# A two-layer hybrid block kernel whose issue order is planned by its own recorder instead of the scheduler

## The chip, the core and the metric

The kernel runs as one launch on one core of a Trainium2 chip. The metric is device microseconds of that launch. Five engines take part, each with its own in-order instruction queue: TensorE (PE in the profile) multiplies, VectorE (DVE), ScalarE (ACT) and GpSimd (POOL) do elementwise work, and SyncE (SP) issues the DMAs. An instruction at the head of a queue that waits for another engine holds up everything behind it on its own engine.

## The reference

The model is a diffusion block of two layers on 512 tokens and 256 context tokens, width 1024, feed-forward width 4096. Layer 1 carries no context queries. What is computed, cut to its skeleton:

```python
for each of the 2 layers:
    shift1, scale1, gate1, shift2, scale2, gate2 = silu(c) @ mod_w + mod_b     # for x and for the context
    h = modulate(rmsnorm(x), shift1, scale1)
    u = h @ w_in                                                              # split over four mixers
    y = concat(ssd_mixer(u), diff_mixer(u), gqa_mixer(u), mla_mixer(u))       # 256 columns each
    x = x + gate1 * (y @ w_out)
    h = modulate(rmsnorm(x), shift2, scale2)
    x = x + gate2 * (square(relu(h @ w1)) @ w2)
return rmsnorm(x) * final_norm_g
```

The four mixers are a chunked state-space scan in both directions, a differential attention (two softmaxes subtracted), a grouped-query attention and a latent attention, each with four heads; the three attentions run over 768 keys (context and tokens).

## The kernel before

Activations are held transposed, 128 features by 768 tokens, in eight tiles. Each large product is kept near float32 by splitting both factors into a high and a low part, and summing three products: high by high, high by low, low by high. `split` makes the parts of a weight: a copy on ScalarE (line 393), then a subtraction on VectorE or GpSimd (line 394). All products go through `mm` (line 198), transposes are on line 765.

The tiles named below: `pv` are the value projections, `pdk`, `pdq`, `pgb`, `pcqx` and their like the other input projections (`p` and the column group), `d_`, `g_` and `m_` the three attentions, with `_s` scores, `_t` transposed probabilities, `_o` outputs; `pe`, `pg`, `py`, `pst`, `hs` belong to the scan; `p` alone is the feed-forward. `pm`, `pn`, `pk` and `pl` are the modulation: `pm` multiplies the condition by a block of `mod_w` in four column groups of 32, `pn` sums the four, line 282 adds the bias into `modT`, line 366 forms the gain, lines 555 to 561 apply gain and shift and leave `xn` in high and low parts, which `pv` multiplies. Line 275 copies `pm` out of PSUM as `ms`. `pk` (loaded as `mk`) is the same for the later modulation columns of layer 0, spread between other work.

Products with a 64- or 32-column weight (`_o`, `pk`, `pm`, `py`, `pst`, `pg`) use part of the array's columns each (the profile writes 128*64 and 128*32); all others use it in full (128*128).

Stages in time: the start (norm, first modulation, value projections) to 58.5 us; projections and mixers of layer 0, with its modulation columns, to about 520; output projection and feed-forward of layer 0 to about 1100, beside which VectorE computes layer 1's modulation (line 312); the same for layer 1, mixers from about 1200 to 1510, feed-forward to the end, then the final norm (`nf_`, line 1425) and the store. While the last feed-forward products run, line 1308 adds each to the residual `h`, emptying its PSUM tile, and `squares` sums the squares into `acc` (line 522, on GpSimd, the eighth and last on VectorE), from which `nf_ms` is multiplied.

What sets the order. In the mixers, several Python generators (attention, projections, scan, modulation) are interleaved by `Weave`, which steps the one whose clock is least; the weights of that clock stand in `TUNE`. The instructions so traced are then ordered by the framework's scheduler, which simulates the engines with its own durations, takes priorities from `high_priority(e[4])` in `Weave.run`, and gives out pool buffers as it goes. Two things are held by hand: the start, from the norm to the last `pv`, stands in a `manual_schedule` block for PE, ScalarE and VectorE; and `issue_after` keeps the `pk` products behind the last product traced. PSUM has two score tiles of 1024 columns (tag `S`) and four of 512 (tag `g`).

Of the kernel before, what the change touches and what calls it, by code (L numbers as in the profile page):

```python
# [12 lines left out]
F32R = mybir.dt.float32r  # L13
# [6 lines left out]
P = 128  # L20
D = 1024
KT = 8
# [46 lines left out]
    pass  # L69


class Weave:


# [43 lines left out]

@with_exitstack
def hybrid_block_kernel(ctx: ExitStack, tc: tile.TileContext, a: dict, out: bass.AP, dbg=None):  # L120
    nc = tc.nc
    nc.scalar.preload_act_table_set("natural_log_exp_and_others")

    sb = ctx.enter_context(tc.tile_pool(name="sb", bufs=1))
    pp = ctx.enter_context(tc.tile_pool(name="pp", bufs=1, space=PSUM))
    dp = ctx.enter_context(tc.tile_pool(name="dp", bufs=1, space=DRAM))

    NL, NSM, NP, NWR, NWS, NSD = 43, 4, 6, 7, 4, 3

# [64 lines left out]
    stt = nc.vector.scalar_tensor_tensor  # L194
    gtt = nc.gpsimd.tensor_tensor
    gts = nc.gpsimd.tensor_scalar
    def mm(*args, **kw):
        r = nc.tensor.matmul(*args, **kw)  # L198
        K.last = r.ins
        return r  # L200

    ld = nc.sync.dma_start

    def f(ap):
# [14 lines left out]


    ident = const("ident", [P, P])
    make_identity(nc, ident)
    ones = const("ones", [P, P])
    nc.gpsimd.memset(ones, 1.0)
    epsT = const("epsT", [P, 1])
# [90 lines left out]
    def mod_quads():  # L316
# [20 lines left out]
        for i in range(4 * n):  # L337
            load(i + 1)
            yield 1.6 if i % 4 == 0 else 0.8
            if i % 4 == 0:  # L340
                po = ps_g(f"pk{i}")
            with tc.issue_after(K.last):
                for k in (2 * (i % 4), 2 * (i % 4) + 1):
                    w = ws.pop((i, k))
                    for g in range(4):
                        mm(po[32 * g : 32 * g + 32, 0:P], sil[:, k], w[:, P * g : P * g + P], start=k == 0, stop=k == KT - 1)
            if i % 4 == 3:
                m = sc(f"mq{i}", P)
                act(m, po[:, 0:P], AF.Copy)
                yield 0.2  # L350
                with tc.issue_after(K.last):
                    spread(i // 4, m)

    LO0 = nc.gpsimd.scalar_tensor_tensor
    LOP = ()
# [231 lines left out]
            except StopIteration as e:  # L587
                return e.value

    with tc.manual_schedule(engines={mybir.EngineType.PE, mybir.EngineType.Activation, mybir.EngineType.DVE}):  # L590
        for i, s in enumerate((XS, CS)):
            run(rstd_of(f"n1_0_q{i}", psq[i], rb, s))
        ws = [value_of(wv[0])]
        mod_done(0, mod_load(0))
        xn_start(0)
        ws.append(value_of(wv[1]))
        m = mod_load(1)
        mod_dma(3)
        next(wv[3])
        vps = v_start(0)  # L600
        for q in range(4):
            run(v_step(0, vps, ws[q], xn, 2 * q))
            if q < 3:
                mod_done(q + 1, m)
                xn_start(q + 1)
            if q < 2:
                ws.append(value_of(wv[q + 2]))
            run(v_step(0, vps, ws[q], xn, 2 * q + 1))
            if q < 2:
                m = mod_load(q + 2)  # L610


    tri = const("tri", [P, 2, P])
# [701 lines left out]
    for l in range(DEPTH):  # L1315
# [214 lines left out]
```

## Time and profile before

| | |
|---|---|
| median of 3 runs | 1863.81 us (1862.91 to 1869.71) |
| the profiled execution | 1864.9 us, of which the span is 1863.2 us |
| TensorE busy in the span | 1781.6 us, 96% |
| TensorE not busy | 81.6 us |
| mean granted TensorE clock | 0.982 of full speed |
| VectorE, ScalarE, GpSimd busy | 1088.6, 872.2, 465.8 us |

The profile is one execution. A busy time is the union of an engine's instructions; matmuls are pipelined, so a row's duration is longer than the distance to the next row, and the distance between two starts is what a matmul costs. The granted clock takes two values, full (2.4 GHz) and half (1.2 GHz), and a stretch's clock is their mean.

### The profile page before, as it was taken

Reading aid. Unit: us, or ns where it says so; the run is one execution under the profiler, and the core shown is the slowest. Engines: PE = TensorE matmul, PEld = TensorE weight load, DVE = VectorE, ACT = ScalarE, POOL = GpSimd, SP = SyncE. Lnnn points to the kernel's source line nnn. Section 1 sums busy time; section 2 is a strip of 40 time slices with the busy share of each in tenths; the row PEclk is TensorE's granted clock in tenths of the full one; section 3 lists DMA queues with packets and bytes.
Section 4 is the critical chain, followed back from the end, with each engine's and each line's share of the span. In section 5 each row is a group of like instructions: output and inputs, shape, how many; then the busy total and the mean of one; then the engine's idle time right before and its main releaser. Section 6 shows DMA issues by size and latency. Waiting matters only on the chain.

```text
span 1863.2 us, 30142 instructions
## 1 busy us (share of the span) xinstructions
PE 1781.6 (96%) x11206; PEld 1485.9 (80%) x11206; DVE 1088.6 (58%) x2112; ACT 872.2 (47%) x1776; POOL 465.8 (25%) x437
## 2 busy tenths in 40 slices
PE   7989999899999999999999999998899999999996
PEld 5777686677787988888888889787678998888885
DVE  5366856867485764543543265887986863333324
ACT  5245665767455313213213353676777652323242
POOL 2322322220134301101001674242211320101065
PEclk9989999999999999999999999999999999999998
DMA  9365422014345543432433334522014552332333
GB/s 356 106 166 162 111 74 62 27 25 150 95 131 153 174 138 97 151 126 91 147 125 100 127 119 116 137 73 65 13 48 152 168 166 91 96 96 92 96 119 102
DMA packets 117330, 216.28 MB, mean 116 GB/s; under 512 B 15424, under 2 KB 24640, under 8 KB 117184
## 3 DMA queue, kind: packets, MB, share of 16 engines
q1 hardware_dynamic: 117184, 214.36, 37.4%
q8 instruction: 88, 1.44, 0.3%
q14 instruction: 58, 0.48, 0.1%
HBM read 185.99 MB, written 8.13 MB: 104 GB/s over the span
## 4 chain that ended last, share of the span: by engine, by line
PE 82%; DVE 8%; ACT 4%; POOL 3%; issue 2%; DMA 1%; DVEq 0%; SPq 0%; POOLq 0%; ACTq 0%
PE p L198 45%; PE po L198 3%; PE pdk L198 2%; PE pv L198 2%; PE m_s L198 2%; PE pr L198 2%; PE m_o L198 2%; PE pdq L198 2%; PE d_o L198 2%; PE m_t L765 1%; PE g_o L198 1%; PE pk L198 1%; PE pxs L198 1%; PE g_s L198 1%; PE pe L198 1%
## 5 line engine op out<-in xcount | busy, mean ns | idle before, releaser
L393 ACT ACTIVATE w_0s<-w 128x512 fp32r<-128x512 f32 x256 | 160.9, 630 | 394.0 <-PE p L198 354.3
L1384 POOL TENSOR_TENSOR r<-r 128x512 f32<-128x512 f32 (+2 forms) x80 | 91.9, 1148 | 652.9 <-ACT a_0h L1383 387.9
L394 DVE TENSOR_TENSOR w_0s<-w,w_0s 128x512 fp32r<-128x512 f32 x216 | 150.6, 698 | 165.6 <-ACT w_0s L393 165.4
L312 DVE SCALAR_TENSOR_TENSOR junk<-mv,cb 128x512 bf16<-128x512 f32 x128 | 91.4, 718 | 117.6 <-DMA mv<-in_modw_dram 116.5
L1382 ACT ACTIVATE r<-p 128x512 f32<-128x512 f32 (+2 forms) x80 | 47.8, 597 | 168.6 <-PE p L198 166.9
L1308 DVE SCALAR_TENSOR_TENSOR h<-p,modT,h 128x512 f32<-128x512 f32 (+1 forms) x104 | 62.6, 624 | 102.2 <-PE p L198 102.2
L749 DVE TENSOR_REDUCE d_m<-d_s 128x1 f32<-128x768 f32 (+1 forms) x80 | 65.8, 842 | 33.4 <-PE d_s L198 33.3
L753 ACT ACTIVATE d_p<-d_s,d_m 128x768 f32<-128x768 f32 (+1 forms) x80 | 64.7, 812 | 35.6 <-DVE d_m L749 27.8
L394 POOL TENSOR_TENSOR w_0s<-w,w_0s 128x512 fp32r<-128x512 f32 x40 | 53.2, 1337 | 39.8 <-ACT w_0s L393 38.6
L522 POOL TENSOR_TENSOR acc<-acc,sq 128x256 f32<-128x256 f32 (+1 forms) x48 | 49.5, 1031 | 42.3 <-ACT sq L521 40.6
L198 PE MATMUL p<-xm_0h,w_0s 128*128 128x512 f32 (+1 forms) x176 | 55.1, 360 | 1.9 <-ACT r L1382 1.9
L198 PE MATMUL p<-a_0h,w_0s 128*128 128x512 f32 (+1 forms) x176 | 54.6, 356 | 0.9 <-DVE h L1308 0.5
L198 PE MATMUL p<-a_4h,w_0s 128*128 128x512 f32 (+1 forms) x176 | 54.6, 355 | 0.0
L198 PE MATMUL p<-xm_4h,w_0s 128*128 128x512 f32 (+1 forms) x176 | 54.6, 357 | 0.0
L198 PE MATMUL p<-xm_6h,w_0s 128*128 128x512 f32 (+1 forms) x176 | 54.5, 357 | 0.0
L198 PE MATMUL p<-xm_2h,w_0s 128*128 128x512 f32 (+1 forms) x176 | 54.4, 356 | 0.0
L198 PE MATMUL p<-a_2h,w_0s 128*128 128x512 f32 (+1 forms) x176 | 54.3, 355 | 0.0
L198 PE MATMUL p<-xm_7h,w_0s 128*128 128x512 f32 (+1 forms) x176 | 54.3, 356 | 0.0
L198 PE MATMUL p<-a_6h,w_0s 128*128 128x512 f32 (+1 forms) x176 | 54.3, 355 | 0.0
L198 PE MATMUL p<-xm_3h,w_0s 128*128 128x512 f32 (+1 forms) x176 | 54.3, 355 | 0.0
L198 PE MATMUL p<-xm_5h,w_0s 128*128 128x512 f32 (+1 forms) x176 | 54.2, 355 | 0.0
L198 PE MATMUL p<-a_7h,w_0s 128*128 128x512 f32 (+1 forms) x176 | 54.1, 353 | 0.0
(2380 smaller groups left out, 5625.0 us busy)
## 6 DMA issues: line engine op xcount, KB each, us to landing
w<-in_w_dram SPq DMA_DIRECT2D x320, 256.0 KB, 2.6
mv<-in_modw_dram SPq DMA_DIRECT2D x96, 256.0 KB, 2.7
mk<-in_modk_dram SPq DMA_DIRECT2D x64, 256.0 KB, 3.4
wr<-in_wout_dram SPq DMA_DIRECT2D x32, 256.0 KB, 2.8
h<-in_xT_dram SPq DMA_DIRECT2D x16, 384.0 KB, 7.5
mw<-in_mod_dram SPq DMA_DIRECT2D x16, 384.0 KB, 6.1
wo<-in_wout_dram SPq DMA_DIRECT2D x32, 192.0 KB, 2.4
wv<-in_wv_dram SPq DMA_DIRECT2D x16, 192.0 KB, 4.6
```

The lines of the kernel that those rows point to most:

```text
L198: r = nc.tensor.matmul(*args, **kw)
L312: stt(out=junk, in0=w, scalar=1.0, in1=cb[s, i], op0=ALU.mult, op1=ALU.mult, accum_out=m[:, 2 * i + s : 2 * i + s + 1])
L393: act(hi, src, AF.Copy)
L394: sub(out=lo, in0=src, in1=f(hi), op=ALU.subtract)
L522: (tt if k == KT - 1 else add)(out=acc[:, s], in0=acc[:, s], in1=q[:, s], op=ALU.add)
L749: nc.vector.tensor_reduce(out=u.m[:, 0:1], in_=u.ps[:, 0 : u.n], axis=AX.X, op=ALU.max, negate=True)
L753: act(u.p, u.ps[:, 0 : u.n], AF.Exp, bias=u.m[:, 0:1], accum_out=u.m[:, 1:2])
L765: nc.tensor.transpose(ps[:, i : i + P], u.p[:, b + i : b + i + P], ident)
L1308: stt(out=h[k][:, s], in0=ps, scalar=L.mod[:, mg + k, si : si + 1], in1=h[k][:, s], op0=ALU.mult, op1=ALU.add)
L1382: act(r, ps, AF.Relu)
L1384: gtt(out=r, in0=r, in1=r, op=ALU.mult)
```

## The change

Every engine and pool is replaced by a recorder. An operation is not issued where the program states it, but written down as an `Op` with the operations it must follow, found from the overlap of the tile areas read and written, and with the tiles it needs. Consecutive products into one output tile are joined into one operation as long as their summed duration stays under `GROUP`, 1.0 us. When all is recorded, `order` plays the program through once: each engine takes, of the operations that can start, the one traced first (those on VectorE, ScalarE and GpSimd that touch a PSUM tile of `S` or `g` count as 200 places earlier), buffers are given in the order of tracing, and `issue` then issues everything in that one order, bound on all five engines. Durations come from a table of formulas. The generators, their weights and the arithmetic are as before; the priorities, the `manual_schedule` block of the start and `issue_after` are gone.

```diff
+class Plan:
+    HOP = 0.2
+    EARLY = 200
+    GROUP = 1.0
...
+    def cost(self, eng, name, args, kw, out):
...
+            if w.dt == F32R:
+                return max(0.12, 0.454 * n), 0.17
...
+        self.bytes = 4 * (x.box[1] - x.box[0]) * x.width()
+        return 0.45, 1.2
...
+    def take(self, eng, fn, name, args, kw):
...
+        op = self.ops[-1] if self.ops else None
+        if not (eng == "PE" and op is not None and op.eng == "PE" and op.out is out.t and op.cost + cost <= self.GROUP):
+            op = Op(len(self.ops), eng)
...
+                for box, o in t.writes if not w else t.writes + t.reads:
+                    if o is not op and box[0] < r1 and r0 < box[1] and box[2] < c1 and c0 < box[3]:
+                        op.before.add(o)
...
+    def order(self):
...
+            op.rank = op.n - (self.EARLY if op.eng not in ("PE", "SP") and any(t.tag in ("S", "g") for t in op.tiles) else 0)
...
+            s, e = best
+            op = min((o for o in ready[e] if o.at <= s), key=lambda o: o.rank)
+            ready[e].remove(op)
+            cost = op.cost
+            if e == "POOL":
+                pool = s + cost
+            elif e == "DVE" and pool > s:
+                cost += 0.3 * min(cost, pool - s)
...
+            if e == "SP":
+                dma = max(dma, op.end) + op.bytes / 250e3
+                op.end = max(op.end, dma)
...
+    def issue(self):
...
+        with self.tc.manual_schedule(engines={E.PE, E.Activation, E.DVE, E.Pool, E.SP}):
+            for op in out:
+                for fn, args, kw in op.calls:
+                    i = fn(*[x.real() if isinstance(x, View) else x for x in args],
+                           **{k: x.real() if isinstance(x, View) else x for k, x in kw.items()}).ins
...
-                    if e[4]:
-                        with self.tc.high_priority(e[4]):
-                            c = next(e[2])
-                    else:
-                        c = next(e[2])
+                    c = next(e[2])
...
-    nc = tc.nc
+    real = tc.nc
+    nc = Plan(tc)
...
+    sb = Pool(ctx.enter_context(tc.tile_pool(name="sb", bufs=1)))
...
-            with tc.issue_after(K.last):
...
-    with tc.manual_schedule(engines={mybir.EngineType.PE, mybir.EngineType.Activation, mybir.EngineType.DVE}):
...
+    nc.issue()
```

All issued lines have the number 331 after the change, so rows are told by their tiles. Three places show what moved.

TensorE, where layer 0's projection `pdk` of the second pair of heads meets the modulation products `pk`. Before:

```order
L198 MATMUL pk_711<-mk_0_658,sil 32x128
L198 MATMUL pdk_0_849<-xn_0l,wdk10s_746 128x512
L198 MATMUL pk_711<-mk_1_660,sil 32x128
L198 MATMUL pdk_0_849<-xn_0h,wdk10s_746 128x512
L198 MATMUL pk_711<-mk_1_660,sil 32x128
L198 MATMUL pdk_0_849<-xn_1h,wdk10s_746 128x512
L198 MATMUL pk_711<-mk_1_660,sil 32x128
L198 MATMUL pdk_0_849<-xn_1l,wdk10s_746 128x512
L198 MATMUL pk_711<-mk_1_660,sil 32x128
L198 MATMUL pdk_0_849<-xn_1h,wdk10s_746 128x512
L198 MATMUL pdk_0_849<-xn_2h,wdk10s_746 128x512
```

After:

```order
L331 MATMUL pdq_1_792<-xn_6l,wdq00s_702 128x256
L331 MATMUL pdq_1_792<-xn_6h,wdq00s_702 128x256
L331 MATMUL pk_595<-mk_4_616,sil 32x128 x4
L331 MATMUL pk_595<-mk_5_618,sil 32x128 x4
L331 MATMUL pdq_1_792<-xn_7h,wdq00s_702 128x256
L331 MATMUL pdq_1_792<-xn_7l,wdq00s_702 128x256
L331 MATMUL pdq_1_792<-xn_7h,wdq00s_702 128x256
L331 MATMUL pdk_0_844<-xn_0h,wdk10s_735 128x512
L331 MATMUL pdk_0_844<-xn_0l,wdk10s_735 128x512
L331 MATMUL pdk_0_844<-xn_0h,wdk10s_735 128x512
```

The `pk` products stood one by one between single `pdk` products; they now stand eight together, and the next eight come 18 `pdk` products later.

TensorE in the start, from the fourth block of `pm`. The digit behind `xn_` is the k-tile, that behind `wv_` the weight quarter. Before:

```order
L198 MATMUL pm_453<-mw_1_0_291,sil 32x256 x3
L198 MATMUL pm_453<-mw_1_3_293,sil 32x256 x3
L198 MATMUL pm_453<-mw_1_6_295,sil 32x256 x2
L198 MATMUL pv_0_304<-wv_2s_347,xn_4h 128x384 x2
...
L198 MATMUL pvb_307<-wv_2s_347,xn_4l 128x384
L198 MATMUL pn_490<-sel,ms_470 128x2 x4
L198 MATMUL pv_0_304<-wv_2s_350,xn_5h 128x384 x2
```

After:

```order
L331 MATMUL pm_566<-mw_0_6_337,sil 32x256 x2
L331 MATMUL pm_566<-mw_1_0_368,sil 32x256 x3
L331 MATMUL pm_566<-mw_1_3_376,sil 32x256 x3
L331 MATMUL pm_566<-mw_1_6_380,sil 32x256 x2
L331 MATMUL pn_588<-sel,ms_585 128x2 x4
L331 MATMUL pk_595<-mk_0_239,sil 32x128 x4
L331 MATMUL pk_595<-mk_1_241,sil 32x128 x4
L331 MATMUL pk_595<-mk_2_244,sil 32x128 x4
L331 MATMUL pk_595<-mk_3_246,sil 32x128 x4
L331 MATMUL pv_0_327<-wv_3s_477,xn_6h 128x384 x2
```

Before, the whole `pm` block stood ahead of the `pv` products of k-tiles 4 and 5, with its `pn` between those two; now both stand behind k-tile 5, and only 16 `pk` products are between `pn` and k-tile 6, which needs that block's result.

VectorE in the last microseconds: the residual additions that empty the feed-forward's PSUM tile (`h<-p,modT,h`) and the final norm's products for the first 256 tokens (`h<-h,par,nf_r`). Before:

```order
L1308 SCALAR_TENSOR_TENSOR h_1_14333<-p_3_1_256_18162,modT,h_1_14333 128x256
L1425 SCALAR_TENSOR_TENSOR h_0_14331<-h_0_14331,par,nf_r 128x256
L1425 SCALAR_TENSOR_TENSOR h_1_14333<-h_1_14333,par,nf_r 128x256
L1425 SCALAR_TENSOR_TENSOR h_2_14335<-h_2_14335,par,nf_r 128x256
L1425 SCALAR_TENSOR_TENSOR h_3_14337<-h_3_14337,par,nf_r 128x256
L1425 SCALAR_TENSOR_TENSOR h_4_14339<-h_4_14339,par,nf_r 128x256
L1425 SCALAR_TENSOR_TENSOR h_5_14341<-h_5_14341,par,nf_r 128x256
L1425 SCALAR_TENSOR_TENSOR h_6_14343<-h_6_14343,par,nf_r 128x256
L1425 SCALAR_TENSOR_TENSOR h_7_14345<-h_7_14345,par,nf_r 128x256
L1308 SCALAR_TENSOR_TENSOR h_2_14335<-p_3_2_256_18201,modT,h_2_14335 128x256
L1308 SCALAR_TENSOR_TENSOR h_3_14337<-p_3_3_256_18240,modT,h_3_14337 128x256
```

After:

```order
L331 SCALAR_TENSOR_TENSOR h_1_14343<-p_3_1_256_18146,modT,h_1_14343 128x256
L331 SCALAR_TENSOR_TENSOR nf_r<-nf_q_18183,nf_r 128x256
L331 SCALAR_TENSOR_TENSOR h_0_14341<-h_0_14341,par,nf_r 128x256
L331 SCALAR_TENSOR_TENSOR h_1_14343<-h_1_14343,par,nf_r 128x256
L331 SCALAR_TENSOR_TENSOR h_2_14345<-h_2_14345,par,nf_r 128x256
L331 SCALAR_TENSOR_TENSOR h_2_14345<-p_3_2_256_18189,modT,h_2_14345 128x256
L331 SCALAR_TENSOR_TENSOR h_3_14349<-h_3_14349,par,nf_r 128x256
L331 SCALAR_TENSOR_TENSOR h_4_14356<-h_4_14356,par,nf_r 128x256
L331 SCALAR_TENSOR_TENSOR h_5_14367<-h_5_14367,par,nf_r 128x256
L331 SCALAR_TENSOR_TENSOR h_6_14375<-h_6_14375,par,nf_r 128x256
L331 SCALAR_TENSOR_TENSOR h_3_14349<-p_3_3_256_18232,modT,h_3_14349 128x256
L331 SCALAR_TENSOR_TENSOR h_7_14382<-h_7_14382,par,nf_r 128x256
```

The addition that empties the tile of output 2 stood behind all eight norm products and stands now behind three; that of output 3 stands behind seven.

## Rows read from the trace of the kernel before

**Rows 1.** The page, part 1: busy time, share of the span, instructions.

```profile
PE 1781.6 (96%) x11206; PEld 1485.9 (80%) x11206; DVE 1088.6 (58%) x2112; ACT 872.2 (47%) x1776; POOL 465.8 (25%) x437
```

**Rows 2.** Stretches: length, busy us of each engine, PE clock, DMA share, GB/s.

```profile
0.00:58.50 58.50, 47.44 (x320) 37.76 (x321) 32.50 (x75) 28.85 (x55) 17.08 (x37) 0.97 0.80 297
...
100.00:520.00 420.00, 392.91 (x2800) 302.14 (x2799) 288.48 (x616) 255.23 (x587) 91.31 (x91) 0.96 0.32 94
520.00:1060.00 540.00, 537.72 (x3179) 467.85 (x3180) 283.08 (x576) 166.21 (x279) 107.85 (x82) 1.00 0.41 131
...
1200.00:1510.00 310.00, 296.50 (x2268) 251.74 (x2267) 255.69 (x502) 220.98 (x483) 85.16 (x93) 0.98 0.30 90
...
1786.00:1863.20 77.20, 58.26 (x421) 55.38 (x419) 29.61 (x40) 28.96 (x57) 51.49 (x46) 0.91 0.37 115
```

**Rows 3.** TensorE's waits, whole run: us in total, times, longest us.

```profile
PE d_s L198 <- ACT d_p L753: 6.6, 10, 1.7
PE nf_ms L198 <- DVE acc L522: 5.7, 2, 4.0
PE g_s L198 <- ACT g_p L753: 5.4, 7, 1.8
PE p L198 <- DVE h L1308: 3.8, 2, 3.4
...
PE pk L198 <- DMA mk<-in_modk_dram: 2.5, 2, 1.7
```

**Rows 4.** TensorE in order of time, 160 to 172 us: start, us.

```profile
165.04 0.43 PE L198 MATMUL d_o<-d_pt,dv 128*64 128x128 f32 x2
165.41 0.48 PE L198 MATMUL pcqx<-xn_2h,wcqx0s 128*104 128x512 f32 x1
165.82 0.43 PE L198 MATMUL d_o<-d_pt,dv 128*64 128x128 f32 x2
...
169.27 0.40 PE L198 MATMUL pcqx<-xn_3l,wcqx0s 128*104 128x512 f32 x1
169.50 0.39 PE L198 MATMUL pcqx<-xn_3h,wcqx0s 128*104 128x512 f32 x1
```

**Rows 5.** TensorE in order of time, 452 to 466 us.

```profile
459.37 1.53 PE L198 MATMUL m_o<-m_pt,mv 128*64 128x128 f32 x24
460.83 0.44 PE L765 MATMUL m_t<-ident,m_p 128*128 128x128 f32 x2
...
463.99 0.49 PE L765 MATMUL m_t<-ident,m_p 128*128 128x128 f32 x3
464.42 1.09 PE L198 MATMUL m_o<-m_pt,mv 128*64 128x128 f32 x14
465.44 0.55 PE L765 MATMUL m_t<-ident,m_p 128*128 128x128 f32 x3
```

**Rows 6.** TensorE in order of time, 1833 to 1840 us.

```profile
1838.45 0.36 PE L198 MATMUL p<-a_0h,w_256s 128*128 128x256 f32 x1 [3.36 <-DVE h L1308]
```

**Rows 7.** VectorE in order of time, 1786 to 1864 us.

```profile
1819.36 5.16 DVE L522 TENSOR_TENSOR acc<-acc,sq 128x256 f32<-128x256 f32 x1 [1.16 <-POOL acc L522]
...
1830.07 7.83 DVE L1425 SCALAR_TENSOR_TENSOR h<-h,par,nf_r 128x256 f32<-128x256 f32 x8
...
1852.74 0.42 DVE L522 TENSOR_TENSOR acc<-acc,sq 128x256 f32<-128x256 f32 x1 [0.64 <-ACT sq L521]
```

**Rows 8.** GpSimd in order of time, 1786 to 1864 us.

```profile
1819.28 4.96 POOL L394 TENSOR_TENSOR w_256s<-w,w_256s 128x512 fp32r<-128x512 f32 x4
```

**Rows 9.** ScalarE in order of time, 41 to 54 us.

```profile
44.10 0.60 ACT L275 ACTIVATE ms<-pm 128x512 f32<-128x512 f32 x1 [0.97 <-PE pm L198]
```

**Rows 10.** TensorE in order of time, 37 to 60 us.

```profile
47.23 0.95 PE L198 MATMUL pn<-sel,ms 128*128 128x2 f32 x8
...
52.47 0.44 PE L198 MATMUL pv<-wv_3s,xn_6l 128*128 128x384 f32 x1 [0.65 <-DVE xn_6l L561]
```

**Rows 11.** TensorE in order of time, 86.8 to 91.7 us.

```profile
86.89 0.86 PE L198 MATMUL pk<-mk,sil 128*32 128x128 f32 x24
```

More of the change, by code (lines that the diff above doesn't have):

```diff
@@ new lines, with __init__, ap, box @@
+class Later:
+    def __init__(self, pool, shape, dt, name, tag, bufs):
+        self.args = (pool, shape, dt, name, tag, bufs)
+        self.dt, self.tag, self.bufs = dt, tag, bufs
+        self.made = None
+        self.reads, self.writes = [], []
+        self.left, self.end, self.first, self.last, self.kind, self.slot = 0, 0.0, None, None, None, None
+        self.cols = int(np.prod(shape[1:]))
+        self.base = np.empty(shape, np.int8)
+        self.mem = self.base.__array_interface__["data"][0]
+    def ap(self):
+        pool, shape, dt, name, tag, bufs = self.args
+        if self.made is None and bufs == 1:
+            self.made = pool.tile(list(shape), dt, name=name, tag=tag, bufs=1)
+        elif self.made is None:
+            self.made = pool.tile(list(shape), dt, name=name, tag=f"{tag}_{self.slot}", bufs=1)
+        return self.made
+    def box(self, a):
+        r0, c0 = divmod(a.__array_interface__["data"][0] - self.mem, self.cols)
+        r1, c1 = r0 + 1, c0 + 1
+        for n, s in zip(a.shape, a.strides):
+            if s >= self.cols:
+                r1 += (n - 1) * s // self.cols
+            else:
+                c1 += (n - 1) * s
+        return r0, r1, c0, c1
@@ new lines, with __init__, ask, can @@
+class Tag:
+    def __init__(self, name, bufs):
+        self.name = name
+        self.free, self.queue, self.next = [(0.0, i, None) for i in range(bufs)], [], 0
+    def ask(self, t):
+        self.queue.append(t)
+    def can(self, t):
+        return bool(self.free) and self.queue[self.next] is t
+    def take(self, t):
+        self.next += 1
+        self.free.sort(key=lambda x: x[:2])
+        at, t.slot, t.last = self.free.pop(0)
+        return at
+    def give(self, t):
+        self.free.append((t.end, t.slot, t))
@@ new lines, with __init__, __getattr__, report @@
+class Side:
+    def __init__(self, plan, eng, real):
+        self.plan, self.eng, self.eng_real = plan, eng, real
+    def __getattr__(self, name):
+        fn = getattr(self.eng_real, name)
+        return lambda *args, **kw: self.plan.take(self.eng, fn, name, args, kw)
+def report(out):
+    free, idle = {}, {}
+    for op in out:
+        e = op.eng
+        w = int(op.start // 50)
+        g = op.start - free.get(e, 0.0)
+        idle.setdefault(e, {}).setdefault(w, 0.0)
+        idle[e][w] += g
+        free[e] = op.start + op.cost
+    print("plan ends", max(o.end for o in out), {e: round(sum(o.cost for o in out if o.eng == e), 1) for e in free})
+    for e in ("PE", "DVE", "ACT"):
+        print(e, [round(idle[e].get(w, 0.0), 1) for w in range(40)])
@@ L341, in mod_quads @@
                 po = ps_g(f"pk{i}")
-            with tc.issue_after(K.last):
[L343 to L346, printed above, removed]
+            for k in (2 * (i % 4), 2 * (i % 4) + 1):
+                w = ws.pop((i, k))
+                for g in range(4):
+                    mm(po[32 * g : 32 * g + 32, 0:P], sil[:, k], w[:, P * g : P * g + P], start=k == 0, stop=k == KT - 1)
             if i % 4 == 3:
@@ L588, in value_of @@
                 return e.value
-    with tc.manual_schedule(engines={mybir.EngineType.PE, mybir.EngineType.Activation, mybir.EngineType.DVE}):
[L591 to L610, printed above, removed]
+    for i, s in enumerate((XS, CS)):
+        run(rstd_of(f"n1_0_q{i}", psq[i], rb, s))
+    ws = [value_of(wv[0])]
+    mod_done(0, mod_load(0))
+    xn_start(0)
+    ws.append(value_of(wv[1]))
+    m = mod_load(1)
+    mod_dma(3)
+    next(wv[3])
+    vps = v_start(0)
+    for q in range(4):
+        run(v_step(0, vps, ws[q], xn, 2 * q))
+        if q < 3:
+            mod_done(q + 1, m)
+            xn_start(q + 1)
+        if q < 2:
+            ws.append(value_of(wv[q + 2]))
+        run(v_step(0, vps, ws[q], xn, 2 * q + 1))
+        if q < 2:
+            m = mod_load(q + 2)
     tri = const("tri", [P, 2, P])
```

184 lines of the change are left out of this document (173 added, 11 removed).

## The prediction, made before the changed kernel ran

> **What bounds the kernel now.** I read the shares of the page first: TensorE is busy for 1781.6 of 1863.2 us, so the other 81.6 us are the most that better order of the waits can give, and anything beyond must come out of the busy time [rows 1]. Then the stretches [rows 2]. From 520 to 1060 us TensorE is busy for 537.7 of 540 us at full clock: a feed-forward has nothing to win. The start idles 11.1 us in 58.5, and its transfers run at 297 GB/s. The mixers of layer 0 idle 27.1 us in 420 at a mean clock of 0.96, those of layer 1 13.5 us in 310 at 0.98, with VectorE busy for 255.7 us there, 82%. The end idles 18.9 us in 77.2. Then the waits [rows 3]: no one cause is large; score tiles that wait for the exponentials that free them are 6.6 and 5.4 us, the final norm waits 5.7 us for its sum of squares, the feed-forward's last tiles 3.8 us for VectorE, the modulation 2.5 us for a transfer. Last I read TensorE in order of time for what a busy microsecond contains [rows 4, 5].
>
> **Switches between full and part-column products.** Alternating single `d_o` and `pcqx` products repeat every 0.78 us (165.04 to 165.82) [rows 4]. Alone, a `pcqx` costs 0.23 us (169.27 to 169.50) and two of the trace's `o` rows 0.12 us (24 in 1.46 us, 459.37 to 460.83) [rows 4, 5]. So going into part-column products and back costs 0.78 - 0.35 = 0.43 us. Between transposes it is cheaper: three `m_t` take 0.43 us before an `m_o` block, which then takes 1.02 us for 14 rows, against 0.85 by the 24; with 0.1 us for one transpose (estimated as midway between a quarter of the 0.23, for its 128 columns, and a third of the 0.43), 0.13 + 0.17 = 0.30 us [rows 5].
>
> Counted through the whole order of TensorE, blocks of part-column products fall from 181 to 118. Between full products on both sides they go from 74 to 63, between transposes from 49 to 12, mixed from 58 to 43: 11 x 0.43 + 37 x 0.30 + 15 x 0.36 (the mean of the two) = 21 us. The cause is `GROUP`, which makes neighbours one operation, as in the `pk` place shown. Some of the saved time falls where the next product would have waited anyway. Bounds are half and all of it, 10 and 21 us; I take three quarters, 16, since TensorE idles for only 6% even in the mixers of layer 0 [rows 2].
>
> The Trainium skill's page "TensorEngine Tiling (Array Packing)", Key Properties, says that a change of tiling mode drains the engine. It gives no price; the rows agree with a cost at each change, and by the rule alone the transposes would pay as much as the projections, 63 x 0.43 = 27 us, where the rows make it 21.
>
> **Modulation products waiting for their weights.** After the alternation TensorE waited 2.5 us in two places for `mk` [rows 3]. Four `mk` buffers hold two groups of eight; the new order puts 18 `pdk` products, 18 x 0.23 = 4.1 us, between groups, longer than the wait's longest, 1.7 us. Gain 2.5 us, at the least 0.
>
> **The end.** TensorE stood 3.36 us for the addition that empties a feed-forward tile [rows 6], which was queued behind eight norm products of 7.83 us, 0.98 each [rows 7]. It moves ahead of five of them, 4.9 us, more than the wait: gain 3.4 us. The clock of this stretch is 0.91 [rows 2]; one stall less gives back perhaps 1 us. Together 4.4. The other wait, 4.0 us for `acc` [rows 3], stays: that 0.42-us addition took 5.16 us beside four subtractions of GpSimd that took 4.96 [rows 7, 8], and the same subtractions stand around it in the new order. Bounds 0 (it meets GpSimd again) and 5.5.
>
> **The start pays.** The table loads at 250 GB/s where the trace shows 297 on average [rows 2], so the plan believes the fourth modulation block late and queues it behind k-tile 5. What follows must then run in the open: the copy `ms` (0.60 us, [rows 9]) and 0.1 to reach it, then from the start of `pn` at 47.23 to the first low-part `pv` at 52.47, 5.24 us [rows 10], less the 16 `pk` products put between (24 of them took 0.86 us, so 0.6 [rows 11]). That is 5.3 us, of which about 1 us is `pn` itself, which is work either way, and 0.65 us was idle before [rows 10]: 3.7 us. The third block's `pn` moves one product group later too; I add 0.8. Together -4.5, bounds -2 and -8.
>
> **The waits of the mixers.** Idle there is 27.1 + 13.5 = 40.6 us [rows 2]. In both orders the same operations in nearly the same sequence of units pass the same two score tiles. What is new is the rule that gives anything touching PSUM 200 places, so that in layer 1 the four score maxima that stood behind the 40 small additions of the scan's state now stand ahead of them on VectorE, and the longer waits of `d_s` and `g_s` are of that kind [rows 3]. VectorE at 82% and the chain maximum, exponential, scaling, transpose stay. I take a third, 13 us, with bounds of two thirds, 26, and a loss of 10, since all five queues are now bound and a result that is later than planned holds whatever is behind.
>
> **The clock.** At 0.96 and 0.98 the two mixer stretches ran 0.04 x 420 + 0.02 x 310 = 23 us worth of clock short [rows 2]. The falls follow stalls. With a third of the idle gone I take a quarter, 6 us; bounds 14 gained and 4 lost.
>
> **Where cost is nothing.** Recording adds no instruction; the arithmetic is the same. POOL and SP are now bound too. In the feed-forwards, DMA is busy for 0.41 of the time and TensorE hides all [rows 2]; if a weight came late there, a stall would be a new row.
>
> **The sum.** 16 + 2.5 + 4.4 - 4.5 + 13 + 6 = 37.4 us. Against the profiled execution's 1864.9 us (span 1863.2 and 1.7 around it), 1.1 above the median of the runs, that is 1827.5; I say 1828. All good ends together: 21 + 2.5 + 5.5 - 2 + 26 + 14 = 67, or 1798. All bad ones: 10 + 0 + 0 - 8 - 10 - 4 = -12, or 1877.
>
> **Rivals.** *The waits come back.* If VectorE and ScalarE set the pace in the mixers (82% and 71% busy in layer 1 [rows 2]), a wait removed from one row reappears on another, and neither the 13 us nor the 6 come: 18.4 us, 1846. For it: the waits are many and small [rows 3]. Against: idle is 6% and 4% there, so slack exists on every engine. *The plan is nearly true.* Two thirds of the mixers' idle and most of the clock go, 1864.9 - 64 = 1801; against it stands what the table leaves out, next. *No change.* The saved switches lie in stretches that others pace, the start eats the end's gain: 1862. For it: the orders are alike unit by unit.
>
> *Slower: VectorE held by GpSimd.* The plan charges a VectorE operation only 30% of the time that GpSimd works beside it, while the trace shows 5.16 us for a 0.42-us addition [rows 7]. The plan therefore places products for TensorE just behind VectorE results that arrive up to a whole GpSimd operation late. In the mixers there are 91 + 93 GpSimd instructions of 176.5 us, 0.96 each [rows 2]. A held result costs half of one on average, 0.48 us. It turns my sum into a loss when more than 37.4 / 0.48 = 78 of the 184 hold back a result that TensorE stands for; at 100 it is 48 us, and 1864.9 - 37.4 + 48 = 1875. Against it: the order before was made by a simulation that also had to meet this, and its waits on VectorE are short.
>
> The Trainium skill's page "SBUF — State Buffer", section "Who interferes with whom", has this as an exclusive lock: GpSimd and a VectorE operation that needs the shared port exclude each other for whole instructions. The row of 5.16 us agrees with it and not with the plan's 30%.
>
> **Chances.** Forecast 0.50, waits come back 0.22, nearly true 0.10, no change 0.09, slower 0.09. A measurement of this kernel can tell 0.5%, 9.3 us, from no change. The first three lie beyond it on the fast side, 0.82; I move 0.02 of the second to no change: faster 0.80, same 0.11, slower 0.09. The range leaves out half of the slower case and the outer part of the nearly true one: 1800 to 1863.
>
> **What would show it.** The `pk` products in runs of 16 rows or more and no alternation every 0.78 us; TensorE's busy time lower by 10 to 22 us, the switches; no wait of `p` on line 1308's addition near the end; a new wait of 3 to 4 us of the first `pv` on k-tile 6 before 65 us; mixers shorter by 30 to 40 us in all, with higher clock. It is wrong if busy time does not fall, if the mixers keep over 38 us of idle, or if rows with VectorE as the releaser grow to tens of microseconds beside GpSimd rows.

## The result and the profile after

The changed kernel takes 1814.45 us (1812.52 to 1816.05, four runs) against 1864.43 us of the kernel before: a ratio of 0.9727, interval 0.9703 to 0.975. The profiled execution has a span of 1811.2 us, 52.0 us shorter. Its page, part 1, answers [rows 1]:

```profile
PE 1732.4 (96%) x11206; PEld 1464.8 (81%) x11206; DVE 1085.0 (60%) x2112; ACT 875.6 (48%) x1776; POOL 469.4 (26%) x437
```

TensorE's busy time fell by 49.2 us, its idle time from 81.6 to 78.8 us only. So nearly all of the gain lies inside what the profile calls busy. The next two fences show the mixers, cut where the same work starts in both kernels: from the first score product to the first output projection `pr`, of layer 0 and of layer 1. Columns as in [rows 2]; before, then after:

```profile
101.50:523.50 422.00, 394.34 (x2807) 303.36 (x2806) 290.40 (x618) 257.04 (x590) 94.33 (x93) 0.96 0.32 94
1168.70:1451.30 282.60, 268.29 (x1954) 217.47 (x1953) 230.51 (x454) 201.44 (x440) 77.23 (x81) 0.98 0.28 83
```

```profile
102.70:488.80 386.10, 364.61 (x2811) 293.32 (x2812) 291.61 (x617) 258.28 (x590) 94.14 (x93) 0.98 0.35 104
1134.30:1411.50 277.20, 260.28 (x1953) 214.56 (x1951) 224.18 (x454) 202.69 (x439) 80.16 (x81) 0.98 0.28 81
```

Layer 0's mixers are 35.9 us shorter, 29.7 of it busy time on the same instructions; layer 1's are 5.4 us shorter, and idle more (16.9 us against 14.3). The other large piece is the end: from layer 1's first `pr` to the last instruction it is 12.3 us shorter (411.9 to 399.6), 5.9 of it idle time and 5.1 half clock (defined below). The start is 1.2 us longer, and what lies between the layers the same within 0.4. TensorE's waits after (us in all, times, longest), to be held against [rows 3]:

```profile
PE n_ms L331 <- DVE nlam L331: 9.3, 1, 9.3
PE g_t L331 <- DVE g_p L331: 7.8, 4, 5.8
PE cqn_ms L331 <- ACT cqn_s L331: 4.4, 2, 2.3
PE d_s L331 <- DMA sdq<-hldq_0l: 4.0, 2, 2.3
PE m_s L331 <- ACT m_p L331: 3.9, 6, 1.3
PE d_t L331 <- DVE d_p L331: 3.5, 2, 3.3
...
PE nf_ms L331 <- DVE acc L331: 1.6, 1, 1.6
...
PE g_s L331 <- ACT g_p L331: 1.5, 3, 0.7
...
PE p L331 <- DVE h L331: 0.6, 1, 0.6
...
PE d_s L331 <- ACT d_p L331: 0.3, 1, 0.3
```

The waits of `d_s` and `g_s` for the exponentials fell from 12.0 us to 1.8, but `m_s`, which had no such wait before, has 3.9, so score tiles together still wait 5.7; and transposes that wait for scaled probabilities (`g_t`, `d_t`) stand there with 11.3, one of 5.8 us. In the same view of before these two rows were 3.6 us:

```profile
PE d_t L765 <- DVE d_p L828: 2.0, 1, 2.0
...
PE g_t L765 <- DVE g_p L860: 1.6, 1, 1.6
```

The wait for `mk` is gone; one on `sdq`, a tile that is written to memory and read back, is new.

To split the busy time I went through TensorE's instructions one by one, in every trace. An undisturbed step, from one start to the next at full clock, is in these traces 0.4545 ns per column for a full product, 109 ns for a transpose, 54 ns for a product on half the columns and 27 ns for one on a quarter (two and four such products run at once). What a step takes beyond that is extra time: "blocks" where a part-column product stands on either side of the step, "other" elsewhere. "Half clock" is half of the busy time that lies in stretches at the lower clock. Differences between two rows add up to the difference in span to within 0.5 us. The count of blocks, here and in the prediction, takes in the scan's `pg`. But the profile writes its products 64*128: they use half of the array's rows and all of its columns, other than the kernel's description has it. Without `pg` the blocks fall from 178 to 112. In us:

| kernel | blocks in the order | span | idle | half clock | blocks' extra | other extra |
|---|---|---|---|---|---|---|
| before | 181 | 1863.2 | 81.5 | 25.9 | 66.4 | 47.5 |
| after | 118 | 1811.2 | 78.9 | 17.4 | 34.6 | 38.6 |
| g0_no_group | 144 | 1848.1 | 85.7 | 23.6 | 56.2 | 40.9 |
| split_pk | 157 | 1835.6 | 78.1 | 23.5 | 50.4 | 41.9 |
| strict_trace_order | 113 | 1874.7 | 120.7 | 31.4 | 36.8 | 43.6 |
| early_0 | 122 | 1834.4 | 87.7 | 29.3 | 34.4 | 40.9 |
| flat_table | 116 | 1865.1 | 118.2 | 30.0 | 33.6 | 41.2 |
| only_pe_bound | 118 | 1868.2 | 116.3 | 39.6 | 34.8 | 35.7 |
| three_bound | 118 | 1819.2 | 86.7 | 20.3 | 34.7 | 35.6 |
| g2_group_2 | 112 | 1825.6 | 89.0 | 25.6 | 32.0 | 37.1 |
| dma_340 | 117 | 1810.9 | 80.8 | 15.3 | 35.5 | 37.3 |
| pool_full_charge | 127 | 1850.6 | 97.6 | 37.0 | 36.2 | 38.0 |
| early_probabilities | 120 | 1828.0 | 87.1 | 26.6 | 35.0 | 37.2 |
| hop_021 | 119 | 1823.0 | 87.8 | 21.5 | 35.8 | 36.0 |

Before to after: blocks -31.8, other -8.9, half clock -8.5, idle -2.6. What the other extra is made of no run separates; it is open. In the trace a product in float32 is two rows, so eight `pk` products are 16 rows. Behind the place of the first order shown, the trace of before had 24 and twice eight `pk` rows between waits for `mk`. After, in order of time, they stand in sixteens, 0.58 us from start to start of the next product (90.86 to 91.44), and nothing waits:

```profile
85.60 0.64 PE L331 MATMUL pk<-mk,sil 128*32 128x128 f32 x16
...
90.54 0.40 PE L331 MATMUL pdk<-xn_5h,wdk10s 128*128 128x512 f32 x1
90.86 0.65 PE L331 MATMUL pk<-mk,sil 128*32 128x128 f32 x16
91.44 0.50 PE L331 MATMUL pdk<-xn_6h,wdk10s 128*128 128x512 f32 x1
```

### The profile page after: what moved, and what is told of

Its sections match the earlier page's. It is cut to its first block, busy times and chain, and to the rows that moved or that the text cites. A ratio compares the mean times of both kernels' runs of the same rounds, so it can differ in the third digit from the quotient of the medians.

```text
span 1811.2 us, 30203 instructions
## 1 busy us (share of the span) xinstructions
PE 1732.4 (96%) x11206; PEld 1464.8 (81%) x11206; DVE 1085.0 (60%) x2112; ACT 875.6 (48%) x1776; POOL 469.4 (26%) x437
## 5 line engine op out<-in xcount | busy, mean ns | idle before, releaser
L331 DVE TENSOR_REDUCE d_m<-d_s 128x1 f32<-128x768 f32 (+1 forms) x80 | 66.4, 846 | 34.8 <-PE d_s L331 33.9
L331 POOL TENSOR_TENSOR acc<-acc,sq 128x256 f32<-128x256 f32 (+1 forms) x48 | 49.9, 1041 | 42.3 <-ACT sq L331 41.8
L331 PE MATMUL p<-a_5h,w_0s 128*128 128x512 f32 (+1 forms) x176 | 54.0, 353 | 0.0
L331 PE MATMUL p<-a_3h,w_0s 128*128 128x512 f32 (+1 forms) x176 | 54.0, 353 | 0.0
```

The source lines that it names most:

```text
L331: i = fn(*[x.real() if isinstance(x, View) else x for x in args], **{k: x.real() if isinstance(x, View) else x for k, x in kw.items()}).ins
```

## The experiments

All are edits of the changed kernel. Ratios are to the kernel before, which ran beside each on the same chip; the changed kernel's own is 0.9727 [0.9703, 0.975]. "Slower by" is the difference of a ratio to that, times 1864 us.

**g0_no_group.** `GROUP = 1.0` becomes `GROUP = 0.0`.

> GROUP is 0, so each product is an operation of its own and the plan may put another product between any two. By TensorE's order, blocks of part-column products rise from 118 to 144 (before: 181). Theory A, the saved time is the breaking of part-column blocks: the two traces differ by 63 blocks and 31.8 us of busy time over the nominal step of each product at blocks' entries, exits and inside them, 0.50 us per block; 26 blocks more cost 13 us: 1827 us against 1814 (1822 to 1832), busy time up by 10 to 16 us, idle within 5 us. Theory B, the saved time comes from the planned order as a whole and GROUP hardly matters: 1811 to 1818 us.

Measured: 1850.1 us, ratio 0.9911 [0.9891, 0.9931]; against 0.9727 that is 34 us slower. The direction is A's, the size no one's. The table tells why: 21.6 us of blocks' extra, but also 6.8 of idle and 6.2 of half clock. The last two, 13.0 us together, are no more than the control at the end of this section moves (8.9 and 4.1); the blocks' extra is what the edit did. 26 blocks would cost 0.83 us each, but 13 of the 21.6 us lie at steps inside blocks: by the records of `_o`, `py` and `pst`, steps of under 30 ns, in which a product runs beside the one on other columns, fall from 715 to 630, and those of 80 to 170 ns rise from 649 to 709. Without the group the partners no longer stand next to each other, inside blocks that the count takes for whole. My attribution was also off: GROUP accounts for 26 of the 63 blocks; the other 37 are gone without it, by the planned order alone.

**split_pk.** After the plan is made, every group of eight `pk` calls is cut:

```diff
         out = self.order()
+        ... for each pk operation of 8 calls: up to 3 places behind the next operations of PE,
+        ... none past a reader of its tiles or a reuse of their buffers
+            parts = [op.calls[2 * i : 2 * i + 2] for i in range(4)]
+            op.calls = sum(parts[: 4 - m], [])
+            for i, k in enumerate(reversed(places)):
+                out.insert(k + 1, x)      # x carries parts[3 - i]
```

> The order of the changed kernel, but each group of eight pk calls (16 rows) is issued in up to four pieces of two calls, each piece behind one of the next operations of TensorE, as far as no reader of the result and no reuse of a buffer lies between. Blocks of pk rise from 28 to 69, all blocks from 118 to 157; nothing else is moved. Theory A: 39 blocks at 0.43 us (the alternation's price in the trace of before) to 0.50 us (63 blocks, 31.8 us): 17 to 20 us slower, 1831 to 1834 us, nearly all as busy time of TensorE around pk. Theory B: these products fill time that TensorE would have waited in any case, at most 5 us slower, below 1820 us.

Measured: 1834.04 us, 0.9822 [0.9797, 0.9847], 18 us slower. Theory A holds: 15.8 us more in blocks, 0.41 per block, with idle unchanged (78.9 to 78.1). The profiled execution, the second slowest of five, has 6.1 us of half clock and 3.3 of other extra besides. In its trace, TensorE in order of time:

```profile
129.26 0.63 PE L353 MATMUL pk<-mk,sil 128*32 128x128 f32 x12
129.82 0.61 PE L353 MATMUL d_s<-sdk,sdq 128*128 128x512 f32 x2
130.36 0.41 PE L353 MATMUL pk<-mk,sil 128*32 128x128 f32 x4
130.71 0.61 PE L353 MATMUL d_s<-sdk,sdq 128*128 128x512 f32 x2
```

Four rows alone take 0.35 us (130.36 to 130.71), what ten take in a whole sixteen (0.58 for 16). They are two products, of two rows each, on two of the four column groups, so two groups of columns stand empty, and the way into part-column products and back is paid once more.

**strict_trace_order.** TensorE takes its operations in the order of tracing, ready or not.

```diff
+        lane = [o for o in reversed(self.ops) if o.eng == "PE"]
...
+                if e == "PE":
+                    ops = [o for o in ops if o is lane[-1]]
```

> TensorE takes its operations strictly in the order of tracing, ready or not; the other engines stay with the plan's choice, and GROUP and EARLY are as in the changed kernel. Blocks 113 against 118. Theory A, the gain is TensorE's blocks staying whole, for which the order of tracing suffices: no dearer by blocks, and only the waits that the plan's choice of a ready operation filled come back; the idle of the mixers, 38 us, rises by 5 to 20 us: 1820 to 1835 us, still faster than before. Theory B, the plan's choice by durations carries the gain: 1850 us or more, idle up by over 35 us.

Measured: 1875.98 us, 1.0044 [1.0026, 1.0061], 59 us slower than the change. B, and beyond it: whole blocks (36.8 us of extra, as after) with 41.8 us more idle and 14 more of half clock are worth nothing.

**early_0.** `EARLY = 200` becomes `EARLY = 0`.

> EARLY is 0: operations of VectorE, ScalarE and GpSimd that touch a score or g tile of PSUM stand in the order of tracing and not 200 places ahead. Blocks 122 against 118. The step of the prediction that gave 13 us of the mixers' idle to this rule: the mixers' idle (38 us) rises by about 13 us, 1825 to 1830 us, with more waits of d_s, g_s and m_s for the exponentials. The rival, the waits only change their rows: 1812 to 1819 us.

Measured: 1833.24 us, 0.9813 [0.9789, 0.9837], 16 us slower, 3 us beyond the range expected. Idle in the mixers rose by 7.3 us (38.5 to 45.8), not 13, and the longest waits are not the rows that I had named:

```profile
PE pk L331 <- DMA mk<-in_modk_dram: 10.6, 3, 5.6
PE n_ms L331 <- DVE nlam L331: 9.3, 1, 9.3
PE p L331 <- DVE h L331: 6.3, 2, 5.6
PE d_s L331 <- ACT d_p L331: 3.7, 4, 2.1
...
PE g_s L331 <- ACT g_p L331: 2.9, 7, 0.8
...
PE m_s L331 <- ACT m_p L331: 2.2, 3, 1.0
```

`d_s`, `g_s` and `m_s` cost 3.1 us more than after (8.8 against 5.7), `pk` and `p` 16. So the number came near and the reason did not hold; see hop_021.

**flat_table.** Each operation of ScalarE, VectorE and GpSimd costs its engine's mean in the table.

```diff
-            return 0.17 + 0.85 * n + 0.27 * extra, 0.0
+            return 0.49, 0.0
...
-            return 0.14 + 1.12 * n, 0.0
+            return 0.52, 0.0
...
-            return 0.4 + 1.75 * n, 0.0
+            return 1.07, 0.0
```

> In the table every operation of ScalarE costs 0.49 us, of VectorE 0.52 us, of GpSimd 1.07 us, the means of the trace, whatever its shape; TensorE's and the DMAs' formulas stay, and so GROUP. Blocks 116 against 118. Theory A, the plan works because it knows when each result is there: with flat durations products stand ahead of results that are late, the idle of the mixers (38 us) rises by 15 to 40 us, with 5 to 10 us more at half clock: 1835 to 1860 us. Theory B, any list in which a ready operation goes first does as well, and the numbers matter little: 1811 to 1822 us.

Measured: 1868.3 us, 1.0012 [1.0, 1.0024]. A, at its far end and past it: the whole gain goes. Blocks' extra stays at 33.6, idle rises by 39.3 and half clock by 12.6. Its largest wait is the one of the new kind, grown from 7.8 to 20.4 us:

```profile
PE g_t L325 <- DVE g_p L325: 20.4, 10, 7.7
```

**only_pe_bound, three_bound.** Only TensorE's order is bound; or TensorE's, ScalarE's and VectorE's.

```diff
-        with self.tc.manual_schedule(engines={E.PE, E.Activation, E.DVE, E.Pool, E.SP}):
+        with self.tc.manual_schedule(engines={E.PE}):                              # only_pe_bound
+        with self.tc.manual_schedule(engines={E.PE, E.Activation, E.DVE}):         # three_bound
```

> The plan is made as in the changed kernel, but only TensorE's order is bound; VectorE, ScalarE, GpSimd and SyncE are ordered by the framework's scheduler, traced in the plan's order. TensorE's order is the same, row for row. Theory A, the gain lies in TensorE's own order (whole blocks): 1811 to 1825 us. Theory B, the other queues' order carries the part that early_0 lost (19 us) and more, since a bound TensorE waits for whatever the others put last: 1835 us or more, with the part columns' excess unchanged and the idle up.

> As only_pe_bound, but TensorE, ScalarE and VectorE are bound in the plan's order; only GpSimd and SyncE (which issues the transfers) are left to the framework's scheduler. Theory A, what only_pe_bound lost (51 us) lay in the orders of VectorE and ScalarE, which feed TensorE in the mixers: 1812 to 1822 us, idle within 6 us of the changed kernel's 78.9. Theory B, it lay in the transfers' order or GpSimd's: 1840 us or more, with new waits on DMA rows or POOL rows.

Measured: only_pe_bound 1865.88 us, 1.0004 [0.999, 1.0018]; three_bound 1821.63 us, 0.9761 [0.9741, 0.9781]. The first has TensorE's new order row for row, and is as slow as before. Its mixers:

```profile
101.80:514.90 413.10, 377.38 (x2811) 301.11 (x2811) 290.58 (x617) 258.57 (x589) 96.76 (x93) 0.95 0.33 97
1169.10:1462.90 293.80, 262.37 (x1954) 215.82 (x1953) 223.18 (x453) 203.13 (x439) 79.24 (x81) 0.97 0.25 74
```

TensorE idles for 35.7 and 31.4 us there (after: 21.5 and 16.9). The blocks' 31.6 us are saved and given back as 34.8 of idle and 13.7 of half clock against before (the other extra falls by 11.8). Binding ScalarE and VectorE too brings 45 of the 52 us back, so that is where it was lost; the other 6 are no more than the control below moves.

**g2_group_2, dma_340.** `GROUP = 2.0`; `op.bytes / 340e3` in place of `250e3`.

> GROUP is 2.0 us: an operation of TensorE may hold twice as many products. Blocks 112 against 118. Theory A, price by blocks (0.5 to 0.8 us each, from the changed kernel and from g0_no_group): 3 to 5 us faster, 1809 to 1812 us. Theory B, a larger operation starts only when its last input is there, and what another engine waits for comes later: idle of the mixers up by 3 to 10 us, 1815 to 1825 us.

> The plan's DMA rate is 340 GB/s, not 250. The step of the prediction on the start: at 250 the plan believes the fourth modulation block late and queues it behind k-tile 5, which I priced at 4.5 us; with 340 the start, to the first score product (102.7 us in the changed kernel), is shorter by 3 to 5 us and the whole 1810 us. The rival: TensorE is held by the table's transfers in any case and the order between does not matter: first score product within 1 us, 1813 to 1816 us; above that, the plan now believes later weights early, and TensorE waits for them.

Measured: g2 1827.12 us, 0.9786 [0.9763, 0.9809], slower by 11 us: 2.6 us less in blocks, 10.1 more idle, 8.2 more half clock (B). dma_340 1809.92 us, 0.9702 [0.968, 0.9725]: its interval overlaps the changed kernel's, no difference that can be told. The start is 7.3 us shorter, to 95.4 us, where I had priced 4.5, but not by less idle time. The stretch to the first score product, columns as in [rows 2], in the changed kernel and in dma_340; then the wait that ends it in dma_340:

```profile
0.00:102.70 102.70, 83.36 (x548) 66.84 (x549) 46.62 (x94) 38.91 (x73) 31.04 (x47) 0.95 0.67 223
0.00:95.40 95.40, 76.31 (x539) 61.47 (x539) 48.41 (x94) 38.78 (x73) 31.38 (x47) 0.99 0.71 240
```

```profile
PE d_s L331 <- DMA sdq<-hldq_0h: 6.2, 1, 6.2
```

TensorE idles 19.1 us there against 19.3. The waits of `pv` for `xn` fell from 4.9 us to 0.9, and the first score product waits for `sdq`, on its way through memory, 6.2 us and not 2.3. What makes the start shorter is, for the most part, the clock, 0.99 against 0.95, and ten `pdq` products (0.23 us each) that now stand behind the first score product. Layer 0's mixers are 5.2 us longer. So the planned order lost time in waits at the start, and taking them away brought another wait.

**pool_full_charge.** `cost += 0.3 * min(cost, pool - s)` becomes `1.0 * ...`.

> In the plan a VectorE operation that starts while GpSimd works is charged the whole remaining overlap (up to its own cost) and not 30% of it. Blocks 127 against 118. Theory A (the prediction's rival on the slower side, in small): the plan now expects late VectorE results where they are late, TensorE's waits on VectorE rows fall by 5 to 10 us, which the 9 blocks more at 0.5 us eat in part: 1806 to 1813 us. Theory B, most VectorE operations are not stretched beside GpSimd, the charge makes the table wrong for them, as flat_table did: 1820 us or more, idle up by 5 us or more.

Measured: 1849.77 us, 0.9918 [0.9901, 0.9935], 36 us slower; idle up by 18.7, half clock by 19.6. B; the waits on VectorE rows, which A had falling by 5 to 10 us, rose from 40.4 to 47.1.

**early_probabilities.**

```diff
-any(t.tag in ("S", "g") for t in op.tiles)
+any(t.tag in ("S", "g") or t.args[3].endswith(("_p", "_m")) for t in op.tiles)
```

> The 200 places also for operations on the probabilities and their sums (tiles ending in _p and _m): the scaling of the probabilities and its reciprocal, which stood behind other rows' maxima on VectorE while TensorE waited (g_t for g_p 7.8 us with 5.8 in one wait, d_t for d_p 3.5 us, m_t 0.8 us in the changed kernel). Blocks 120 against 118. Theory A: these 12.1 us fall below 4 us and the whole to 1803 to 1809 us. Theory B, VectorE is simply behind there, and something else of it comes later instead: the g_t and d_t waits go but idle in all stays within 3 us, 1812 to 1818 us.

Measured: 1834.7 us, 0.9833 [0.9814, 0.9851], 20 us slower. The waits of `g_t` and `d_t` for the probabilities went, as A had it, but another came in their place, so that idle rose by 8.2:

```profile
PE pmv L331 <- ACT mv L331: 15.4, 2, 8.8
PE d_s L331 <- ACT d_p L331: 8.6, 7, 3.7
```

Neither theory's number; B's mechanism, with a loss on top.

**hop_021.** `HOP = 0.2` becomes `HOP = 0.21`.

> A control for the experiments that changed one rule of the plan: HOP, the time from one engine's end to another's start, is 0.21 us and not 0.20, a difference that says nothing of the chip. It moves rows all the same: TensorE's order differs from the changed kernel's in 6459 lines, more than with EARLY 0 (5592); blocks 119 against 118. Theory A, the rules carry the time: idle within 4 us of 78.9, 1809 to 1819 us, and the 19 us of early_0 are EARLY's own. Theory B, any other order that the plan gives is worth 10 to 25 us by chance, since the durations are not exact and a queue held in one place shifts the rest: 1824 to 1840 us, with the part columns' excess unchanged (34.6), idle and half clock up; then early_0, g2_group_2 and early_probabilities show no more than this spread.

Measured: 1824.83 us, 0.9772 [0.9748, 0.9797], 8 us slower than the change, at B's lower edge: a setting without meaning moves idle by 8.9 and half clock by 4.1. So differences of 8 us and the like between two plans (g2_group_2's 11, three_bound's 6) can't be put down to the rule that was edited, and of early_0's 16 and early_probabilities' 20 only the part beyond that, if any. The change's own 50 us carry the same doubt: with 0.21 the gain is 42. One control does not give the spread; that stays open. What is at least four times the control's 8 us: 34 us for GROUP, 59 for the choice of a ready operation, 53 for the shapes in the table, 52 for binding the other queues, 36 for the charge.

## Why the prediction was right, and where it was not

The forecast of 1828 us lies 13.6 above the median and the range held it; the gain of 50 us was put at 36. That so wide a range (1800 to 1863) held it owes something to luck, since errors went both ways: the switches and the end gave 16 and 7 us more than said, 8.9 us of other extra stood in no term, and the mixers' idle gave 9.4 less. By its steps, in us of the profiled executions:

| step | said | measured |
|---|---|---|
| switches | -16 (-21 to -10) | blocks' extra -31.8 |
| `mk` wait | -2.5 | gone, -2.5 |
| end | -4.4 (-5.5 to 0) | idle -5.9 (`p` wait -3.2, `nf_ms` wait -4.1), half clock -5.1 |
| start | +4.5 (2 to 8) | idle +5.5, of which 1.8 at the place named; first score product at 102.7 against 101.5 |
| mixers' idle | -13 (-26 to +10) | -3.6 (layer 0 -6.2, layer 1 +2.6) |
| mixers' clock | -6 (-14 to +4) | half clock -4.6 (layer 0 -6.2, layer 1 +1.6) |
| in no term | | other extra -8.9; half clock of the start +1.2 |

*Switches.* The mechanism was right, and the term mis-sized by half. The error is in the price and the discount. I counted blocks and priced their edges; entries and exits gave 18.1 us, near the 21 that I had counted before the discount. But 13.7 us more lie inside the blocks, at steps between two part-column products: a single pair uses part of the columns only, and the others are empty. The alternation of [rows 4] had shown it: two `d_o` rows take 0.37 us there, 0.16 of it by the single records from the first to the second, inside the block, where 0.06 is the mean from row to row in a whole block. I then took off a quarter for time that would be waited in any case; split_pk, the one run that tests it, shows no such discount: its idle did not fall.

The Trainium skill's page "TensorEngine Tiling (Array Packing)", Key Properties, says that different tiles can load weights and multiply in parallel. The rows agree: 16 `pk` rows in 0.58 us after, four in 0.35 us in split_pk. By that rule a broken block loses more than the drain; that second part I had left out.

*Idle in the mixers.* "I take a third, 13 us" is the step that failed. It gave 3.6. A wait taken from one row came back on another (12.0 us of score waits became 5.7, the transposes' 3.6 became 11.3), which is the first rival's mechanism; its 1846 us missed because the blocks gave twice what I said and because of the end. One of the prediction's own signs of being wrong, over 38 us of idle left in the mixers, came true by a hair: 21.5 + 16.9 = 38.4, in stretches cut a little otherwise than those of [rows 2]. Its other sign on busy time, 10 to 22 us less, was passed far (49.2). The reason that I gave, the 200 places, is not shown: early_0's longest waits were others, and of the 7.3 us that its mixers idle more, 3.2 came with the control too (38.5 to 41.7). The larger point is what I did not see: this order of TensorE would by itself cost 35 us of idle (only_pe_bound), and the planned orders of ScalarE and VectorE keep it at the old level. I asked what the new order wins in waits; the right question was what it would lose.

*The end.* The addition stood behind three norm products and TensorE waited 0.6 us for `h`, nearly as worked out. The clock's part, "perhaps 1 us", was 5.1: before, half-clock stretches began at 1825.2 and 1838.9, behind the waits for `acc` and `h`; after, the only one of this stage begins at 1803.3, behind TensorE's last product. That the wait for `acc` would stay was wrong. VectorE and GpSimd at the end, in order of time, answer [rows 7, 8]:

```profile
1774.09 0.59 DVE L331 TENSOR_TENSOR acc<-acc,sq 128x256 f32<-128x256 f32 x1 [0.69 <-ACT sq L331]
...
1781.13 3.70 DVE L331 SCALAR_TENSOR_TENSOR h<-h,par,nf_r 128x256 f32<-128x256 f32 x3
1784.76 0.47 DVE L331 SCALAR_TENSOR_TENSOR h<-p,modT,h 128x256 f32<-128x256 f32 x1
...
1788.24 0.47 DVE L331 SCALAR_TENSOR_TENSOR h<-p,modT,h 128x256 f32<-128x256 f32 x1
...
1804.42 3.26 DVE L331 SCALAR_TENSOR_TENSOR h<-h,par,nf_r 128x256 f32<-128x256 f32 x8
```

```profile
1773.10 9.15 POOL L331 TENSOR_TENSOR w_256s<-w,w_256s 128x512 fp32r<-128x512 f32 x7
```

The addition took 0.59 us, not 5.16, though GpSimd runs the same subtractions from 1773.10 to 1782.25. By the single records it began at 1774.09, GpSimd's subtraction ended at 1774.39, the addition at 1774.67, and the next subtraction, begun at 1774.35, took 1.47 us instead of 1.29. Before, the addition had stood through the running subtraction and three more, and ended 0.29 us after the last. I had taken that one row for a rule.

*The start* has the number and not the place. TensorE idles 5.5 us more than before, and whole `pk` blocks, 5.2 us less extra there, hide most of it. But at the fourth block, which I had priced at 3.7 us, the waits are 0.72, 0.98 and 0.75 us, 1.8 more than the 0.65 of before, and the new wait of 3 to 4 us is not there. `pn` to the first low-part product takes 4.4 us (57.16 to 61.58) where I took 5.24, and the 16 `pk` products between fill 1.1 us and not 0.6: I had read the 24 rows of [rows 11] as 24 products, and they are 12. The rest of the idle time is spread: `n_ms` 1.9 us more, the first `pv` products 2.5, those of k-tile 4 0.7, `sdq` 2.3, against 4.0 that are gone (`mk`, `pl`, and 1.1 of an earlier wait for `ms`).

```profile
57.16 1.05 PE L331 MATMUL pn<-sel,ms 128*128 128x2 f32 x8 [0.72 <-ACT ms L331]
...
60.21 0.62 PE L331 MATMUL pv<-wv_3s,xn_6h 128*128 128x384 f32 x2 [0.98 <-ACT xn_6h L331]
61.58 0.44 PE L331 MATMUL pv<-wv_3s,xn_6l 128*128 128x384 f32 x1 [0.75 <-DVE xn_6l L331]
```

*The slower rival.* Held VectorE results exist, but TensorE's waits on VectorE rows sum to 40.4 us against 36.5 before, nothing like the tens of microseconds more, and a plan that expects every one of them is worse (pool_full_charge). The longest in the mixers, 5.8 us, ends on a VectorE that works through its own queue from 337.69 to 343.01 while GpSimd is still until 341.19: order, not a held result.

## What to carry to other kernels

Products that use part of the array's columns belong together, all column groups side by side: count the blocks in TensorE's order and look at the steps inside them, since this time is shown as busy and no list of waits names it. An order that is better for one engine pays only if the queues that feed it are ordered for it; before judging one, bind it alone and see what comes back as idle. A greedy plan depends on its table, and two settings that mean the same differ by 8 us here, so a single rule is judged only against such controls, and against more than the one made here.

## What the hardware showed

VectorE beside GpSimd is neither slowed by 30% nor always held. The norm product takes 0.41 us when GpSimd is still (3.26 for eight, from 1804.42) and 1.23 when it works (3.70 for three, from 1781.13). The residual addition, which reads PSUM, takes 0.47 in both cases (at 1784.76 GpSimd is still, at 1788.24 it works). Where a VectorE operation was running first, it kept its duration; one that began inside a GpSimd operation ended late. VectorE, then GpSimd, at the end of layer 1's output projection:

```profile
1433.90 1.83 DVE L331 TENSOR_TENSOR w_0s<-w,w_0s 128x512 fp32r<-128x512 f32 x2
...
1436.83 0.68 DVE L331 TENSOR_TENSOR w_0s<-w,w_0s 128x512 fp32r<-128x512 f32 x1
```

```profile
1434.23 0.94 POOL L331 TENSOR_TENSOR acc<-acc,sq 128x256 f32<-128x256 f32 x1 [0.94 <-ACT sq L331]
```

Alone, one subtraction takes 0.68 us; of the two from 1433.90 the first had begun before GpSimd and kept that, and the second, begun at 1434.50 by its record, took 1.23 and ended at 1435.73, 0.56 after GpSimd did. So the two take turns, and how long VectorE is held depends on how many GpSimd operations end before its turn: one here, four in the 5.16 us of [rows 7, 8]. No fixed share in a table says that, neither 30% nor all of the overlap. What decides the turn is open. The Trainium skill's page "SBUF — State Buffer", section "Who interferes with whom", says that a VectorE instruction with two inputs in SBUF contends with GpSimd's reads, and one with at most one, outside the two-port modes, does not. These rows agree; that a VectorE instruction can be passed by several of GpSimd's in a row is only in the trace.

The lower clock came behind pauses of TensorE in every case here, but the sum of idle time does not give its length. split_pk has 0.8 us less idle time than the changed kernel and 23.5 us of half clock against 17.4; just ahead of each of its ten half-clock stretches TensorE had stood for 1.3 to 3.4 us in all. Execution by execution its mean clock goes from 0.983 to 0.989, and the changed kernel's four (0.987 and 0.988) lie between, so these 6 us are not shown to be a cost of the cut blocks. More idle time does go with more half clock: the four kernels with over 97 us of idle (strict_trace_order, flat_table, only_pe_bound, pool_full_charge) have 30 to 40 us of it, the changed kernel 17.4.
